# A hybrid decoder layer on one core: the transfers of a block inversion, side by side and on other queues

## The chip, the cores and the metric

One Trainium2 chip, one of its cores. The metric is the device time of one execution in microseconds (us), lower is better. All data are float32; a product of large matrices is done as three float32r products of parts that are split beforehand into a high and a low half.

## The reference, cut to what matters

One decoder layer runs for a prompt of 256 tokens and for 8 samples of 8 tokens each (320 columns together): adaLN modulation from `w_ada`, one input projection, a gated DeltaNet group and an S5 group beside each other, a GLU on the S5 group, one output projection `w_out`, and a SwiGLU FFN. The change touches the DeltaNet group. There, for each of two chunks of 128 tokens (`c`) and 8 heads, a strictly lower triangular matrix `lmat` is built and the unit lower triangular matrix is inverted:

```
lmat = where(strict, einsum('nbhik,nbhjk->nbhij', kb, kc) * decay, 0)
tinv = triangular_solve(eye + lmat, eye, left_side=True, lower=True)
u = einsum('nbhij,nbhjv->nbhiv', tinv, vc * bc)
```

The heads' outputs are normed, gated by `silu(z)`, and go as the first eight of sixteen row blocks into the product with `w_out`; the other eight come from the S5 group through the GLU.

## The kernel before, in words

**The main stream.** TensorE runs a list of segments. A segment is one weight tile of 512 KB: `load` (L467) brings it in through SP's queue, `do_split` (L496) makes its high half `whi` on ScalarE (L501) and its low half `wlo` on VectorE (L502), and `mm3` (L504) does three products for each of its row blocks. Twelve buffers hold the raw tiles and the halves; at most four segments are split ahead. Segments of `w_ada` (tile `ps_ax`) are used unsplit and are mixed in. In the stretch around the change the list holds, in this order: the GLU with part of `w_ada`; the first half of `w_out` (`first_pair`, `first_half`, the S5 blocks, tile `hT`); then the second half of `w_out` (`second_half`, L2209, the DeltaNet blocks, tile `hz`), which starts only when all eight heads are split (`split_head`).

**The background.** Everything else is written as Python generators that run while the list is put out: after each row block of a segment, `tick` lets every background generator go one step. The order of instructions on each engine is the order in which they are put out, so it is set when the program is built, by a clock of the planner's own: `_run` (L180) books each instruction with a cost, `_dma` (L474) books a transfer with 0.47 us of its queue on SP, 0.1 us on ACT and 1.0 us on POOL and with a time at which it lands, and `fits` (L168) holds a background instruction back until, by these booked times, its inputs are ready. `_start` (L151) gives the time from which an instruction may begin; for an output it also takes the last write of the same tile by another engine, and a DMA counts as another engine. A DMA into a tile that an earlier DMA wrote is therefore put out only when the earlier one has landed by the plan.

**The inversion** (`invert`, L1727) is one of these generators. It runs after the head matrices `L` are built, beside the samples (`samples`, one or two heads at a time). It copies the 32 x 32 diagonal blocks of `L` into `Tc` and sends them to a DRAM scratch `dL`, and zeros to the scratches `dT` and `dW` (6 transfers). Then it reads the 16 x 16 blocks back, regrouped, into `Y` (8 transfers of 16 partitions), solves 128 such blocks at once on VectorE in 15 steps (tiles `P`, `X`, L1770), stores `Y` and `X` to `dW` and `dT` (16 transfers), and loads these as `Wc` and `Tc` (4 transfers). All 34 go through SP's queue, among the weight loads. From there the inverse is put together on TensorE from many 32 x 32 and 64 x 64 products (tiles `ps_bA`, `ps_bB`). Then `chunks` runs for the eight heads, and when these and the samples are done, `split_head` makes `hz`. The inversion holds 7 of the 12 buffers `xw` while it runs.

**What shares the engines it uses.** ScalarE makes the halves `whi`, takes the GLU's gates out of PSUM (`gt`), and serves the samples (`sP`, `kr`, `dk`) and the `w_ada` results (`adaev`). GpSimd (POOL) makes the samples' masks `Z` and `sP` and sums squares (`sqa`).

Of the kernel before, what the change touches and what calls it, by code (L numbers as in the profile page):

```python
# [110 lines left out]
class Layer:  # L111
# [36 lines left out]
            e += x * (n - 1)  # L148
        return [(nm, i) for i in range(f // g, e // g + 1)]

    def _start(self, eng, outs, ins, same):  # L151

        t = 0.0
        rd, la = self.rd, self.la
        for ap in ins:
            for k in self._keys(ap):
                r = rd.get(k)
                if r:
                    t = max(t, r[0] + (same if r[1] == eng else 0.2))
        for ap in outs:  # L160
            for k in self._keys(ap):
                for r in (rd.get(k), la.get(k)):
                    if r and r[1] != eng:
                        t = max(t, r[0] + 0.2)
                t = max(t, self.war.get(k[0], 0.0) + 0.2)
        return t

    def fits(self, eng, outs, ins):  # L168

        c = self.clk  # L170
        t = self._start(eng, outs, ins, 0.0)
        if eng == "PE":
            return t <= c["now"] + self.EPS_PE
        return (eng == "SP" or c[eng] <= c["now"] + self.LIM) and t <= max(c[eng], c["now"]) + self.EPS
# [505 lines left out]
    def xw(self, name="xw"):  # L680
        return self._slot(self.mp.tile([128, 356], F32, name=name, tag="xw", bufs=self.CAP["xw"]), "xw", self.CAP["xw"])

    def dma(self, out, in_, eng=None):
        n = 1
        for d in out.shape:
            n *= d
        q = "SP" if eng in (None, self.nc.sync) else "ACT" if eng is self.nc.scalar else "POOL"
        if self.dry:
            self.sig = q, (out,), (in_,)
            return  # L690
        self.stage_end = max(self.stage_end, self._dma(q, n, out, in_))
        return (eng or self.nc.sync).dma_start(out, in_)
# [1034 lines left out]
    def invert(self):  # L1727

        nc, V, G = self.nc, self.V, self.G
        L = self.L  # L1730
        q_ = nc.sync
        yield from self.take("xw", 7)
        yield from self.take("t4")
        v = lambda t: t[:, :256].rearrange("p (h q) -> p h q", h=8)
# [1 line left out]
        dL, dT, dW = (self.dp.tile([4, 32, 16, 32], F32, name="inv%d" % i) for i in range(3))  # L1736
        Tc = [self.xw("Tc") for _ in range(2)]
        Wc = [self.xw("Wc") for _ in range(2)]
# [7 lines left out]
        yield  # L1746
        flat = lambda d: d.rearrange("b r (c h) q -> c (b r) (h q)", c=2)
        for c in range(2):
            yield from self.p.dma(flat(dL)[c], Tc[c][:, :256], q_)
            for d in (dT, dW):  # L1750
                yield from self.p.dma(flat(d)[c], Wc[0][:, :256], q_)
        G.memset(X[:, 0:256:17], 1.0)
        G.memset(T, 0.0)
        yield
# [1 line left out]
        Yv = Y[:, :256].rearrange("p (r q) -> p r q", r=16)  # L1756
        blk = lambda d, s, b: d[b, 16 * s:16 * s + 16, :, 16 * s:16 * s + 16].rearrange("r h q -> h r q")
        for s in range(2):
            for b in range(4):
                p0 = 64 * s + 16 * b  # L1760
                yield from self.p.dma(Yv[p0:p0 + 16], blk(dL, s, b), q_)
        yield
        yield from self.p.ts(Y[:, :256], Y[:, :256], -1.0, OP.mult)
        for i in range(1, 16):
# [10 lines left out]
        for t, d in ((Yv, dW), (Xv, dT)):  # L1775
            for s in range(2):
                for b in range(4):
                    p0 = 64 * s + 16 * b
                    yield from self.p.dma(blk(d, s, b), t[p0:p0 + 16], q_)
        yield  # L1780
        for t, d in ((Wc, dW), (Tc, dT)):
            for c in range(2):
                yield from self.p.dma(t[c][:, :256], flat(d)[c], q_)
        yield
        Pt = [X, Y]

# [868 lines left out]
```

## Time and profile before

| | |
|---|---|
| median of 3 runs | 1825.05 us |
| lowest, highest | 1821.77, 1828.55 us |
| the profiled execution's own time | 1823.18 us |
| its span, first to last instruction | 1821.4 us |
| TensorE matmul busy | 1731.8 us, 95% of the span |
| VectorE, ScalarE, GpSimd busy | 987.7, 768.9, 335.0 us |
| mean granted TensorE clock | 0.977 of full |

The profile is of one execution. Busy times overlap between engines. Where a view says that an engine waited for "issue", it waited for nothing that the profile shows. A matmul's own duration is longer than its share of TensorE's time, because matmuls are pipelined; a product of 320 columns starts each 0.15 us or so while its row says 0.31 us. SPq, ACTq and a POOL row with DMA_DIRECT2D are instructions that start a transfer; their duration is the issue, not the transfer.

### The profile page before, as it was taken

The page shows a single profiled execution, that of the slowest core. Times are in us where ns is not written, and L with a number is a line of the kernel's source. Part 1 is how long each engine was busy: PE and PEld are TensorE (multiplying, and loading weights), DVE is VectorE, ACT ScalarE, POOL GpSimd, SP SyncE. Part 2 cuts the span into 40 slices and gives each one's busy share as a digit, 9 for nine tenths or more (in the row PEclk, how much of TensorE's full clock was granted, in tenths as well). Part 3 has the DMA queues.
Part 4 walks back from the last instruction along what each step waited for, and adds up shares of the span by engine and source line. Part 5 has one row for each costly group of instructions (what it writes and reads, how often), then busy time and mean ns, then how long its engine had stood idle before and what let it go on. Part 6 is the DMA issues. An engine that isn't in the chain of part 4 may idle for free.

```text
span 1821.4 us, 32727 instructions
## 1 busy us (share of the span) xinstructions
PE 1731.8 (95%) x12961; PEld 1600.4 (88%) x12961; DVE 987.7 (54%) x1840; ACT 768.9 (42%) x1439; POOL 335.0 (18%) x439
## 2 busy tenths in 40 slices
PE   7899998898999889997999999999999999999997
PEld 4678997776787769995999999999999999999997
DVE  3587842788865556677633434444443444444455
ACT  3433334677744434664433333333333333333343
POOL 1000185556132212065300000000000000000043
PEclk8999998999999989998999999999999999999998
DMA  8898744776858956758465565554565545655452
GB/s 275 297 369 287 193 111 129 230 217 209 262 172 257 301 172 179 225 165 289 128 185 174 150 183 169 149 150 122 153 176 151 151 119 152 180 150 149 117 154 80
DMA packets 501262, 340.66 MB, mean 187 GB/s; under 512 B 45355, under 2 KB 452619, under 8 KB 500781
## 3 DMA queue, kind: packets, MB, share of 16 engines
q1 hardware_dynamic: 483904, 332.41, 59.5%
q10 hardware_dynamic: 16838, 5.93, 1.3%
q8 instruction: 102, 1.67, 0.4%
q14 instruction: 50, 0.41, 0.1%
q0 software_dynamic: 368, 0.24, 0.1%
HBM read 323.22 MB, written 14.54 MB: 185 GB/s over the span
## 4 chain that ended last, share of the span: by engine, by line
PE 67%; DVE 3%; ACT 1%; issue 1%; DMA 1%; ACTq 0%; SPq 0%; DVEq 0%
PE ps_mm L319 34%; PE ps_bA L319 17%; PE ps_bB L319 14%; PE ps_ax L319 2%; DVE acc L281 1%; DVE wlo L502 1%; PE ps_bA L333 1%; ACT hT L264 0%; DVE u L281 0%; PE ps_mm L333 0%; DVE P L281 0%; DMA inv<-Y 0%; DMA raw<-in_w_ada_dram 0%; ACT whi L501 0%; DMA S<-in_state_delta_dram 0%
## 5 line engine op out<-in xcount | busy, mean ns | idle before, releaser
L502 DVE TENSOR_TENSOR wlo<-raw,whi 128x1024 fp32r<-128x1024 f32 (+2 forms) x441 | 502.6, 1142 | 554.3 <-ACT whi L501 327.2
L501 ACT ACTIVATE whi<-raw 128x1024 fp32r<-128x1024 f32 (+2 forms) x441 | 424.4, 965 | 412.3 <-DVE wlo L502 309.4
L319 PE MATMUL ps_mm<-h,whi 128*128 128x320 f32 x1376 | 303.4, 308 | 0.0
L319 PE MATMUL ps_mm<-hT,whi 128*128 128x320 f32 x1204 | 290.6, 328 | 2.9 <-ACT hT L264 1.5
L319 PEld LDWEIGHTS ps_mm<-h,whi 128*128 128x128 f32 x1376 | 229.9, 187 | 0.8 <-issue 0.8
L319 PEld LDWEIGHTS ps_mm<-hT,whi 128*128 128x128 f32 x1204 | 202.8, 193 | 14.9 <-issue 6.2
L319 PE MATMUL ps_mm<-h,wlo 128*128 128x320 f32 x688 | 211.6, 307 | 0.0
L319 PE MATMUL ps_mm<-hT,wlo 128*128 128x320 f32 x602 | 189.2, 314 | 2.2 <-DVE wlo L502 2.2
L319 PE MATMUL ps_bA<-h,whi 128*128 128x320 f32 x736 | 166.3, 313 | 3.2 <-DVE h L281 3.0
L319 PE MATMUL ps_bB<-h,whi 128*128 128x320 f32 x704 | 156.0, 309 | 0.0
L319 PE MATMUL ps_mm<-f,whi 128*128 128x320 f32 x704 | 155.5, 308 | 0.0
L281 POOL TENSOR_TENSOR sqa<-acc 128x320 f32<-128x320 f32 x1 | 0.7, 722 | 841.1 <-DVE acc L281 841.1
L319 PEld LDWEIGHTS ps_bA<-h,whi 128*128 128x128 f32 x736 | 125.9, 192 | 4.5 <-DVE h L281 3.3
L319 PEld LDWEIGHTS ps_mm<-h,wlo 128*128 128x128 f32 x688 | 128.9, 187 | 0.0
L319 PEld LDWEIGHTS ps_bB<-h,whi 128*128 128x128 f32 x704 | 118.4, 189 | 0.8 <-issue 0.8
L319 PEld LDWEIGHTS ps_mm<-hT,wlo 128*128 128x128 f32 x602 | 115.5, 192 | 3.5 <-DVE wlo L502 3.5
L319 PEld LDWEIGHTS ps_mm<-f,whi 128*128 128x128 f32 x704 | 117.3, 187 | 0.8 <-ACT whi L501 0.8
L319 PE MATMUL ps_bA<-h,wlo 128*128 128x320 f32 x368 | 115.1, 313 | 1.7 <-DVE wlo L502 1.7
L319 PE MATMUL ps_mm<-f,wlo 128*128 128x320 f32 x352 | 108.5, 308 | 0.4 <-DVE wlo L502 0.4
L319 PE MATMUL ps_bB<-h,wlo 128*128 128x320 f32 x352 | 108.6, 308 | 0.0
L319 PE MATMUL ps_ax<-raw,cs 128*32 128x512 f32 (+2 forms) x832 | 99.6, 588 | 6.9 <-DMA raw<-in_w_ada_dram 6.9
L319 PE MATMUL ps_mm<-hx,whi 128*128 128x320 f32 x328 | 81.1, 333 | 3.3 <-ACT whi L501 3.3
(594 smaller groups left out, 2900.7 us busy)
## 6 DMA issues: line engine op xcount, KB each, us to landing
raw<-in_w_ada_dram SPq DMA_DIRECT2D x180, 512.0 KB
raw<-in_w_gate_dram SPq DMA_DIRECT2D x88, 512.0 KB
raw<-in_w_up_dram SPq DMA_DIRECT2D x88, 512.0 KB
raw<-in_w_in_dram SPq DMA_DIRECT2D x66, 512.0 KB
raw<-in_w_down_dram SPq DMA_DIRECT2D x64, 512.0 KB
raw<-in_w_out_dram SPq DMA_DIRECT2D x32, 512.0 KB
raw<-in_w_down_dram SPq DMA_DIRECT2D x64, 192.0 KB
raw<-in_w_glu_dram SPq DMA_DIRECT2D x16, 512.0 KB
```

The costliest lines, as they stand in the source:

```text
L281: return e.tensor_tensor(out, a, b, op=op)
L319: return self.T.matmul(out, lhsT, rhs, start=start, stop=stop)
L333: return self.T.transpose(out, in_, self.ident[b:b + p, b:b + p])
L501: return (self.S.activation(s.hi[:, :w], s.raw[:, :w], AF.Copy), self.V.tensor_tensor(s.lo[:, :w], s.raw[:, :w], s.hi[:, :w].bitcast(F32), ...
L502: self.V.tensor_tensor(s.lo[:, :w], s.raw[:, :w], s.hi[:, :w].bitcast(F32), op=OP.subtract))
```

## The change

The `beside` flag of a transfer takes one rule out of the planner: its output need not wait for the landing of an earlier DMA into the same tile. All 34 transfers of `invert` get it. The six first transfers and the sixteen stores are issued by ScalarE (`qs`), the eight loads of `Y` stay on SP (`q_`), and the four last loads are issued by GpSimd (`ql`). No arithmetic, no transfer and no buffer is added or taken away.

```
-    def _start(self, eng, outs, ins, same):
+    def _start(self, eng, outs, ins, same, dma=False):
...
-                    if r and r[1] != eng:
+                    if r and r[1] != eng and not (dma and r[1] == "DMA" and r is rd.get(k)):
...
     def fits(self, eng, outs, ins):
         c = self.clk
-        t = self._start(eng, outs, ins, 0.0)
+        dma = eng[-1] == "*"
+        eng = eng.rstrip("*")
+        t = self._start(eng, outs, ins, 0.0, dma)
...
-    def dma(self, out, in_, eng=None):
+    def dma(self, out, in_, eng=None, beside=False):
...
-            self.sig = q, (out,), (in_,)
+            self.sig = q + "*" * beside, (out,), (in_,)
...
-        q_ = nc.sync
+        q_, qs, ql = nc.sync, nc.scalar, nc.gpsimd
...
-            yield from self.p.dma(flat(dL)[c], Tc[c][:, :256], q_)
+            yield from self.p.dma(flat(dL)[c], Tc[c][:, :256], qs, beside=True)
             for d in (dT, dW):
-                yield from self.p.dma(flat(d)[c], Wc[0][:, :256], q_)
+                yield from self.p.dma(flat(d)[c], Wc[0][:, :256], qs, beside=True)
...
-                yield from self.p.dma(Yv[p0:p0 + 16], blk(dL, s, b), q_)
+                yield from self.p.dma(Yv[p0:p0 + 16], blk(dL, s, b), q_, beside=True)
...
-                    yield from self.p.dma(blk(d, s, b), t[p0:p0 + 16], q_)
+                    yield from self.p.dma(blk(d, s, b), t[p0:p0 + 16], qs, beside=True)
...
-                yield from self.p.dma(t[c][:, :256], flat(d)[c], q_)
+                yield from self.p.dma(t[c][:, :256], flat(d)[c], ql, beside=True)
```

## Rows read from the trace of the kernel before

**Rows 1.** The page: busy time by engine, and the chain that ended last by engine.
```profile
PE 1731.8 (95%) x12961; PEld 1600.4 (88%) x12961; DVE 987.7 (54%) x1840; ACT 768.9 (42%) x1439; POOL 335.0 (18%) x439
...
PE 67%; DVE 3%; ACT 1%; issue 1%; DMA 1%; ACTq 0%; SPq 0%; DVEq 0%
```

**Rows 2.** Windows (us: length, PE PEld DVE ACT POOL busy; clock, DMA share, GB/s).
```profile
560.00:580.00 20.00, 19.62 (x148) 15.52 (x148) 10.28 (x23) 9.98 (x17) 4.42 (x8) 1.00 0.96 302
580.00:600.00 20.00, 18.82 (x131) 14.93 (x130) 14.62 (x40) 5.53 (x8) 5.52 (x8) 1.00 0.97 322
600.00:620.00 20.00, 18.01 (x137) 14.94 (x139) 8.35 (x23) 8.77 (x15) 4.79 (x8) 1.00 0.88 270
...
640.00:660.00 20.00, 16.42 (x338) 12.95 (x338) 14.16 (x30) 10.86 (x20) 4.57 (x6) 1.00 0.89 280
660.00:680.00 20.00, 14.94 (x413) 13.40 (x414) 9.53 (x26) 4.19 (x12) 2.92 (x7) 0.74 0.33 95
```

**Rows 3.** Waits of PE, 550 to 770 us (total, times, longest).
```profile
PE ps_bB L319 <- issue: 8.0, 2, 4.7
PE ps_mm L333 <- ACT gt L264: 3.1, 2, 1.7
...
PE ps_bA L319 <- DMA S<-in_state_delta_dram: 0.3, 1, 0.3
```

**Rows 4.** The scratch tiles `inv`: issue times ns min/median/max, first and last start.
```profile
L692 SPq DMA_DIRECT2D Y<-inv x8: 328/528/1863, 559.5 to 579.2; - x8
L692 SPq DMA_DIRECT2D inv<-Y x8: 327/644/1988, 601.1 to 626.8; - x8
L692 SPq DMA_DIRECT2D inv<-X x8: 423/559/1892, 627.7 to 642.1; - x8
...
L692 SPq DMA_DIRECT2D Wc<-inv x2: 376/526/675, 642.9 to 643.7; - x2
L692 SPq DMA_DIRECT2D Tc<-inv x2: 320/372/424, 646.7 to 647.1; - x2
```

**Rows 5.** Timeline of DVE, 556 to 603 us (start, duration).
```profile
585.69 1.23 DVE L502 TENSOR_TENSOR wlo<-raw,whi 128x1024 fp32r<-128x1024 f32 x1 [0.94 <-ACT whi L501]
586.83 0.29 DVE L299 TENSOR_SCALAR Y<-Y 128x256 f32<-128x256 f32 x1
...
600.68 0.39 DVE L274 COPY Y<-X 128x256 f32<-128x256 f32 x1
```

**Rows 6.** The tile `Wc`, its first use on PE.
```profile
L319 PE MATMUL ps_bA<-Wc,L x128: 191/191/212, 648.2 to 649.3; 32*32 32x32 f32 x128
```

**Rows 7.** The head tiles `hz`: first products, and their low halves on DVE.
```profile
L319 PE MATMUL ps_mm<-hz,whi x256: 307/308/387, 769.1 to 826.5; 128*128 128x320 f32 x128
...
L281 DVE TENSOR_TENSOR hz<-z,hz x8: 481/484/485, 764.6 to 768.9; 128x320 fp32r<-128x320 f32 x8
```

**Rows 8.** Transfers issued by ACT, of the tiles `so` and `co`.
```profile
L692 ACTq DMA_DIRECT2D out_dram<-so x6: 337/355/437, 498.0 to 503.6; - x6
...
L692 ACTq DMA_DIRECT2D out_dram<-co x12: 746/804/872, 337.1 to 490.4; - x12
```

**Rows 9.** Timeline of ACT, 556 to 602 us, with the idle time before.
```profile
568.34 0.31 ACT L264 ACTIVATE sP<-kr 64x128 f32<-64x128 f32 x1 [5.19 <-PE ps_bA L319]
...
601.76 0.31 ACT L264 ACTIVATE sP<-kr 64x128 f32<-64x128 f32 x1 [5.11 <-issue]
```

**Rows 10.** Timeline of POOL at the start: transfers that it issues.
```profile
1.32 0.71 POOL L560 DMA_DIRECT2D vr<-in_b_ada_dram  x1 [0.86 <-DVE wr L562]
...
2.52 0.49 POOL L566 DMA_DIRECT2D wr<-in_g_post_mix_dram  x1
```

**Rows 11.** Windows of 4 us after the stop in the inversion's products.
```profile
660.00:664.00 4.00, 1.51 (x127) 1.37 (x128) 0.00 (x0) 0.00 (x0) 0.00 (x0) 0.64 0.98 282
664.00:668.00 4.00, 1.80 (x29) 1.32 (x28) 1.31 (x4) 0.00 (x0) 0.00 (x0) 0.50 0.19 53
668.00:672.00 4.00, 4.00 (x27) 3.80 (x26) 3.93 (x11) 0.39 (x1) 0.00 (x0) 0.58 0.00 0
```

## The prediction, made before the changed kernel was run

> **What bounds the kernel now.** I read the page first: TensorE's matmuls cover 95% of the span, and the chain that ended last is 67% TensorE, 1% DMA [rows 1]. So a change that moves no product can pay only where TensorE stands still or runs at a lower clock. The windows show how much that is around the change: in the five that stand there (of the stretch 560 to 680 us, less 620 to 640) TensorE is busy 19.62, 18.82, 18.01, 16.42 and 14.94 of 20 us, 12.2 us short together [rows 2]. Next I asked what TensorE waited for between 550 and 770 us. The longest is "issue", 8.0 us in two stops, then a gate on ScalarE with 3.1 us; the only DMA in the list is a state load of the samples with 0.3 us, and neither a scratch tile of the inversion nor a weight tile stands there [rows 3]. So the inversion's transfers are slow, but TensorE does not wait for them: it has the GLU and the first half of `w_out` to do.
>
> How slow, the tile's own view says: eight loads of `Y` spread over 19.7 us (559.5 to 579.2), sixteen stores over 41.0 us (601.1 to 642.1), four loads to 647.1 [rows 4]; the first product that uses them starts at 648.2 [rows 6]. And who waits for the end of it: the heads' tiles `hz`. Their last low half is made from 768.9 to 769.4 us, and the first product with `hz` starts at 769.1 [rows 7]. The heads are ready in the moment in which TensorE gets to them. Making them earlier makes nothing earlier unless TensorE also gets there earlier.
>
> **The change, part by part.**
>
> *The eight loads of `Y`, let go side by side.* By the median issue of 0.528 us they take 8 x 0.528 = 4.2 us [rows 4], from 559.5 to 563.7. Before, the last issue (579.2) was 7.6 us ahead of the first VectorE instruction on `Y`, at 586.8 [rows 4, 5]; with the same distance the solve starts at 571.3, 15.5 us earlier. On TensorE that is worth nothing. The risk is that VectorE stands at this instruction, because the plan takes it as ready sooner than the queue, full of weights, delivers; behind it in VectorE's order stand the `wlo` halves, 1.23 us each [rows 5]. Bounds: 0 to 3 us lost. I take 0, since the 7.6 us before held other VectorE work and no stop that reached TensorE.
>
> *The solve* is unchanged: 586.8 to 601.1, 14.2 us [rows 5], so now to 585.5.
>
> *Sixteen stores (and the six first transfers) through ScalarE.* What SP is rid of, 22 issues of some half a microsecond, gains nothing, as no weight tile is waited for [rows 3]. What ScalarE gets is 16 issues in a row in the GLU. ScalarE's own transfers took 0.355 us (`so`, whole rows) and 0.804 us (`co`) [rows 8], the same stores on SP 0.644 and 0.559 us with a backlog in the queue, at least 0.327 [rows 4]. So 16 x 0.355 = 5.7 to 16 x 0.804 = 12.9 us; I take 0.5 us, nearest to SP's smallest values and `so`, and get 8 us. In this time ScalarE makes no `whi` and takes no gate out of PSUM. The cover can be read: ScalarE stood still for 5.19 us before 568.34 and for 5.11 us before 601.76 [rows 9], and TensorE's list of waits has nothing that answers to these. ScalarE is otherwise light here, 5.53 of 20 us busy [rows 2]. So about 5 us are hidden: 8 - 5 = 3 us would show if the stores came in one block; the plan puts some other ScalarE work between them, since it lets ScalarE run only about 1 us ahead of its clock. I take 2 us. Bounds: 5.7 - 5 = 0.7, and with breaks nothing, to 12.9 - 5 = 7.9 us.
>
> *The four last loads through POOL.* POOL's issues took 0.49 to 0.71 us [rows 10], four of them 2.0 to 2.8, against 1.8 on SP by its medians (2 x 0.526 + 2 x 0.372) [rows 4]: no difference by itself. What counts is the wait. They must wait for the landing of the stores, POOL works in order, and behind them stand the samples' masks, for which TensorE's sample products wait. And the inversion's first product on TensorE, placed by the plan, then stands in front of all the GLU's products if `Wc` is late. The plan books 0.1 us for a ScalarE issue, so 1.6 us for sixteen, where I expect 8: `Wc` and `Tc` come some 6 us later than the plan has them. Part of that TensorE has already lost at ScalarE (2 us), and the real clock runs behind the plan's: a product of 320 columns is booked with 0.136 us and takes 0.148. Over the 29 us between the first load of `Y` and the end of the stores that gives back 29 x 0.09 = 2.6 us. Left is 6.4 - 2 - 2.6 = 1.8 us; I take 1. Bounds: 0 to 12.9 - 1.6 = 11.3 us.
>
> *The products of the inversion, moved.* With stores from 585.5 to 593.5, some 3 us of landing, 2 us of loads and 1.5 us until use, the first product comes at about 600 us instead of 648.2, and all that follows it about 45 us earlier. The products are the same, and so, I think, is their stop: twice TensorE waited for "issue" in a run of 256 tiny products, and then it ran at a clock of 0.64, 0.50 and 0.58 (half speed is 1.2 instead of 2.4 GHz) for the next 12 us [rows 3, 11]. The DMA share is 0.89 around the stop before and 0.97 and 0.88 around the new place [rows 2], so I see no reason for it to shrink. I take 0. Bounds: the stop goes, -8.0 us, and with it the low clock: the busy 1.51 + 1.80 + 4.00 = 7.3 us at a mean of 0.57 would be 7.3 x 0.43 = 3.1 us shorter, so -11.1; or a third stop, +4.7 [rows 3].
>
> *The heads, 45 us earlier.* Their chains and the samples fill other gaps of TensorE's order; the seven `xw` buffers come free sooner, so two samples run together earlier. `hz` would be ready in the 730s, and TensorE still gets to it when the first half of `w_out` is through, near 770. What the earlier end gives is slack, 0 us.
>
> **The sum**, against the profiled execution's own 1823.18 us (span 1821.4, 1.8 us around it): 0 + 0 + 2 + 1 + 0 + 0 = +3, so 1826 us. The profiled execution is 1.9 us below the median of the runs and inside their spread of 1821.77 to 1828.55, so I leave it there.
>
> **Rivals.**
>
> *The stop in the tiny products goes or shrinks*: 1823.2 - 11.1 = 1812 us. For it: the first run of 128 tiny products at 648.2 had no stop, it is over by 649.5 [rows 6]; where the runs fall between the other products is new. Against it: the two stops came in runs that are put out in one piece, and they still are. Chance 0.18.
>
> *Slower: TensorE stands in front of `ps_bA<-Wc,L`.* One mechanism: ScalarE's issues take 0.8 us as `co` did, the stores end 11.3 us after the plan's time, POOL holds the loads that long, and TensorE, in order, waits. It costs 11.3 us and then the low clock that followed 8.0 us of stops, 3.1 us: 1823.2 + 14.4 = 1838 us. It decides from about 0.6 us an issue on (16 x 0.6 = 9.6, more than the 5 us of cover and the 2.6 us of drift together). For it: the stores are 16 partitions in pieces of 64 bytes, not whole rows. Against it: SP issued the same pieces in 0.33 to 0.42 us at best [rows 4], and ScalarE's own queue holds no weights. Chance 0.18.
>
> *POOL's loads are held up by VectorE.* If each of the four has to wait out one `wlo`, the longest thing VectorE does there, it is 4 x 1.23 = 4.9 us [rows 5] in front of TensorE: 1828 us. No row of before shows POOL issuing beside such work. The Trainium skill ("SBUF — State Buffer", "SBUF: two separate sides") says that GpSimd cannot write the descriptors of its transfers while VectorE holds the port that the two share, and that such a transfer took 3100 ns instead of 620; by an estimate from these figures the four would come 4 x 2.5 = 10 us late. Chance 0.05.
>
> *The transfers are late anyway.* The 16 DMA engines are 96 and 97% busy here, at 302 and 322 GB/s [rows 2]; if the loads and stores wait behind weights, they end little earlier and the plan's order changes without effect: 1823 us. The Trainium skill ("DMA: Bandwidth & Descriptors", "Issuing engines are not separate DMA queues") says that transfers started by different engines run on the same 16 DMA engines, and that more issuing engines save issue time alone. Against it: most of the 41 us of the stores is the plan's spacing, 16 issues by their medians are 8 x 0.644 + 8 x 0.559 = 9.6 us [rows 4]. Chance 0.15.
>
> **How the numbers follow.** The forecast has 0.44, with a range of its own of 1819 to 1833. About 0.5%, 9 us, is what a measurement of this kernel can tell from no change. The first rival is faster by more than that (0.18), the second slower by more (0.18); the forecast, the third and the fourth lie within (0.64). The range goes from 1814, near the first rival's time, to 1836, near the second's.
>
> **What would show it.** Right: no wait of TensorE on `Wc` above 2 us; the first `ps_bA<-Wc,L` near 600 us; `hz` made some 30 us or more ahead of its first product; that product still near 770. ScalarE's issues: 0.36 to 0.6 us each, with PE waiting for `whi` or `gt` 2 to 3 us more than before. The stop for "issue", two times 3 to 5 us, at the new place. Wrong: the stop gone (then the first rival), a wait of 5 us or more on `Wc` or on a mask (the second or third), the first product on `Wc` not before 630 us (the fourth), or the first product on `hz` well away from 770 for a reason not in this list.

## The result, and the profile after

The kernel after takes 1836.07 us (median of 14 runs, 1829.92 to 1847.01), the one before 1823.85 us in the same measurement (14 runs, 1816.45 to 1828.55): ratio 1.007, interval [1.0054, 1.0087]. It is 12.2 us (0.7%) slower, where the forecast was +3 us and a change of less than 0.5%, and lies at the upper end of the range of 1814 to 1836. The profiled execution of after took 1837.29 us, with a span of 1835.5 us.

The page of after, busy time and chain by engine, against [rows 1]:

```profile
PE 1736.9 (95%) x12961; PEld 1602.8 (87%) x12961; DVE 987.5 (54%) x1840; ACT 770.2 (42%) x1441; POOL 333.8 (18%) x443
...
PE 75%; DVE 8%; DMA 6%; POOL 4%; ACT 4%; issue 2%; SPq 1%; ACTq 0%; DVEq 0%; POOLq 0%
```

The instruction counts of TensorE and VectorE are the same. TensorE is busy 5.1 us longer, and the ledger below puts that to the low clock; the span grew by 14.1 us, so it also stood still for longer. The transfers themselves did what the change says. The scratch tiles `inv` in after (issue times in ns, first and last start), against [rows 4], and the first use of `Wc` with the heads' products, against [rows 6, 7]:

```profile
L694 SPq DMA_DIRECT2D Y<-inv x8: 303/447/521, 565.2 to 569.6; - x8
L694 ACTq DMA_DIRECT2D inv<-Y x8: 309/432/671, 585.4 to 591.7; - x8
L694 ACTq DMA_DIRECT2D inv<-X x8: 309/460/594, 592.2 to 597.7; - x8
...
L694 POOL DMA_DIRECT2D Wc<-inv x2: 538/578/617, 603.7 to 604.3; - x2
L694 POOL DMA_DIRECT2D Tc<-inv x2: 538/538/538, 604.9 to 605.5; - x2
```
```profile
L321 PE MATMUL ps_bA<-Wc,L x128: 191/191/212, 609.2 to 610.3; 32*32 32x32 f32 x128
```
```profile
L321 PE MATMUL ps_mm<-hz,whi x256: 304/308/387, 780.6 to 840.3; 128*128 128x320 f32 x128
...
L283 DVE TENSOR_TENSOR hz<-z,hz x8: 481/482/484, 746.5 to 749.3; 128x320 fp32r<-128x320 f32 x8
```

Sixteen stores start within 12.3 us instead of 41.0, the first product on `Wc` comes 39 us earlier, and the heads are ready at 749.8 us. But TensorE gets to them at 780.6 instead of 769.1: they now lie ready for 31 us. Where TensorE lost this is in its list of waits, 550 to 770 us, against [rows 3]:

```profile
PE ps_bA L321 <- DVE kr L301: 9.5, 3, 8.5
PE ps_bA L321 <- issue: 3.0, 2, 2.6
PE ps_bA L321 <- DVE L L283: 2.3, 2, 1.8
PE ps_mm L321 <- DVE wlo L504: 1.4, 2, 0.7
PE ps_mm L335 <- ACT gt L266: 0.8, 1, 0.8
```

One stop of 8.5 us is new. Its chain is read backwards through three timelines (start, duration, idle time before and what ended it): TensorE waits for `kr`, VectorE makes `kr` from `ps_bA`, by a factor for which it waits for `sP` on ScalarE, and ScalarE is issuing stores.

```profile
589.61 0.44 PE L335 MATMUL ps_bA<-ident,xcat 128*128 128x128 f32 x2
...
590.63 0.31 PE L321 MATMUL ps_mm<-hT,wlo 128*128 128x320 f32 x1
599.39 1.19 PE L321 MATMUL ps_bA<-sP,kb 128*128 128x128 f32 x4 [8.46 <-DVE kr L301]
```
```profile
588.27 0.22 DVE L283 TENSOR_TENSOR Z<-xcat,sx 128x64 f32<-128x64 f32 x1
598.64 0.60 DVE L301 TENSOR_SCALAR kr<-ps_bA,dk 64x128 f32<-64x128 f32 x2 [10.15 <-ACT sP L266]
```
```profile
586.15 0.43 ACT L266 ACTIVATE gt<-ps_mm 128x320 f32<-128x320 f32 x1
586.38 5.75 ACTq L694 DMA_DIRECT2D inv<-Y  x6
592.17 5.95 ACTq L694 DMA_DIRECT2D inv<-X  x8
598.23 0.38 ACT L266 ACTIVATE sP<-ps_bA 128x256 f32<-128x256 f32 x1 [11.65 <-DMA raw<-in_w_ada_dram]
```

Fourteen stores stand in one piece in ScalarE's order and hold it for 11.74 us. The mean of 0.84 us from one start to the next hides how: one row lasts 0.31 to 0.67 us, and between some of the rows ScalarE stood still. The timeline, asked for 586.3 to 590 and for 590 to 592.1 us, shows the longest of these standstills, 2.8 us after the fifth of the sixteen stores:

```profile
586.38 1.61 ACTq L694 DMA_DIRECT2D inv<-Y  x3
590.83 1.31 ACTq L694 DMA_DIRECT2D inv<-Y  x3
```

Three more, of 0.25, 0.75 and 1.42 us, stand ahead of the 12th to the 14th store. The four make 5.2 of the 11.74 us; the fourteen issues by themselves take 0.46 us each. No row of ScalarE says what it waited for, but the queues show what was moved meanwhile (packets, MB, share of the 16 DMA engines; q1 holds what SP issued, q10 what ScalarE issued), from 585.4 to 588.5 and from 588.5 to 590.83 us:

```profile
q1 hardware_dynamic: 726, 1.26, 105.8%
...
q1 hardware_dynamic: 715, 0.62, 78.2%
q10 hardware_dynamic: 1360, 0.08, 39.7%
```

All sixteen stores are 4352 packets, so five are 1360. While weights filled the DMA engines, nothing of the five issued stores was moved, and ScalarE issued the sixth when all of the five had been. The same is seen in e4 and e6 below (2.8 and 3.2 us after the fifth store, on again behind 1360 packets) and in e3 (1.9 us after the sixth, on again behind 1632, which is six stores). In e1 and e5 SP issued the sixteen 0.49 us apart without a standstill; there SP had issued no weight tile for 5.2 us before them, and the DMA engines were 30% busy (e1, 586 to 592 us). So the rows put the standstills down to stores that could not move, and not to the price of an issue. No run removes the standstills alone, and why ScalarE stops at five or six is not shown.

The view says that `sP` waited for a weight tile; that is the last semaphore it saw, and the rows above it show what filled the time. What the stop did to the clock is in the windows of 4 us (length, PE PEld DVE ACT POOL busy; clock, DMA share, GB/s), against [rows 11]:

```profile
588.00:592.00 4.00, 2.94 (x32) 2.28 (x30) 0.46 (x3) 0.00 (x0) 0.00 (x0) 1.00 1.06 290
592.00:596.00 4.00, 0.00 (x0) 0.00 (x0) 0.00 (x0) 0.00 (x0) 0.00 (x0) 0.66 1.04 268
596.00:600.00 4.00, 0.61 (x3) 0.64 (x4) 0.60 (x2) 0.38 (x1) 0.00 (x0) 0.50 1.02 286
600.00:604.00 4.00, 4.00 (x19) 4.00 (x19) 0.77 (x2) 0.83 (x3) 1.87 (x3) 0.56 0.48 134
...
628.00:632.00 4.00, 3.82 (x135) 3.42 (x135) 1.81 (x5) 3.80 (x11) 1.21 (x5) 0.50 0.84 233
632.00:636.00 4.00, 4.00 (x34) 3.67 (x34) 0.86 (x4) 1.03 (x3) 0.52 (x1) 0.50 0.30 107
636.00:640.00 4.00, 4.00 (x33) 2.15 (x35) 1.64 (x2) 1.43 (x2) 1.04 (x3) 0.50 0.34 85
```

Half clock (0.50, so 1.2 GHz) until about 603 us behind the stop, and again from 628 to 640, behind the products of the inversion.

**A ledger.** From the first copy into `Tc` to the last product on `hz` TensorE has the same products to do in every kernel here. I cut this stretch into windows of 2 us and added up, in each, idle time (length less PE busy) and low clock (PE busy times one less the granted clock). What is left, the work at full clock, is 253.5 us before and 253.6 after.

| stretch | before: length, idle, clock | after: length, idle, clock |
|---|---|---|
| copy to first product on `Wc` | 93.9, 6.5, 0.0 | 52.7, 10.1, 2.1 |
| the inversion's products | 35.0, 8.4, 2.9 | 34.7, 5.5, 6.7 |
| to the first product on `hz` | 85.9, 0.5, 0.0 | 136.7, 3.4, 0.0 |
| products on `hz` | 57.7, 0.6, 0.0 | 60.0, 2.8, 0.0 |
| sum | 272.5, 16.1, 2.9 | 284.1, 21.8, 8.8 |

The 11.6 us more of this stretch are 5.7 of idle time and 5.9 of low clock. The piece on ScalarE is 8.5 + 2.1 = 10.6 of it; the products lose 12.2 instead of 11.3; the heads' stretch loses 2.2 more; the rest is some 2 better. Whether that makes the piece the cause is what the experiments were for.

### The profile page after: what moved, and what is told of

Same layout as the page of the kernel before. It is cut to its first block, busy times and chain, and to the rows that moved or that the text cites. A ratio compares the mean times of both kernels' runs of the same rounds, so it can differ in the third digit from the quotient of the medians.

```text
span 1835.5 us, 32725 instructions
## 1 busy us (share of the span) xinstructions
PE 1736.9 (95%) x12961; PEld 1602.8 (87%) x12961; DVE 987.5 (54%) x1840; ACT 770.2 (42%) x1441; POOL 333.8 (18%) x443
## 4 chain that ended last, share of the span: by engine, by line
PE 75%; DVE 8%; DMA 6%; POOL 4%; ACT 4%; issue 2%; SPq 1%; ACTq 0%; DVEq 0%; POOLq 0%
PE ps_mm L321 37%; PE ps_bA L321 20%; PE ps_bB L321 15%; PE ps_ax L321 2%; POOL bx L283 2%; DVE wlo L504 2%; DVE ca L308 1%; ACT whi L503 1%; DMA raw<-in_w_out_dram 1%; POOL AB L283 1%; DMA raw<-in_w_in_dram 1%; DMA ts<-ts 1%; POOL ctab L283 1%; PE ps_bB L335 1%; SPq L474 1%
```

## The experiments

Each was timed in five rounds beside the kernel before, whose median was 1821.7 to 1824.1 us from one measurement to the next; so the differences are to be compared, not the medians. "Stretch" is the length of the ledger's stretch in its one profiled execution, "excess" its idle time and low clock.

| run | median, us | above before, us | ratio, interval | stretch less 272.5 | excess |
|---|---|---|---|---|---|
| after | 1836.07 | +12.2 | 1.007 [1.0054, 1.0087] | +11.6 | 21.8 + 8.8 |
| e1 all on SP | 1831.61 | +9.2 | 1.0049 [1.0036, 1.0061] | +8.0 | 21.5 + 4.9 |
| e2 queues, no flag | 1835.99 | +13.6 | 1.0079 [1.0059, 1.0099] | +8.4 | 20.9 + 4.8 |
| e3 issue booked | 1834.70 | +12.3 | 1.0064 [1.0045, 1.0083] | +12.2 | 22.5 + 9.0 |
| e4 last loads on SP | 1845.31 | +22.9 | 1.0124 [1.0098, 1.0151] | +24.0 | 28.8 + 14.3 |
| e5 held, SP | 1840.85 | +16.8 | 1.0098 [1.007, 1.0125] | +14.1 | 20.0 + 11.4 |
| e6 held, ScalarE | 1838.71 | +14.7 | 1.0084 [1.0056, 1.0113] | +15.3 | 25.3 + 8.6 |
| e7 before, 16 cuts | 1830.77 | +6.7 | 1.0043 [1.0026, 1.0059] | +4.7 | 16.3 + 1.7 |
| e8 chunks held | 1832.58 | +8.5 | 1.005 [1.0031, 1.0069] | +9.6 | 22.2 + 7.7 |
| e9 after's plan, SP | 1832.86 | +9.8 | 1.0049 [1.0032, 1.0066] | +9.2 | 19.4 + 9.1 |
| e10 before's plan, new queues | 1827.08 | +4.0 | 1.0019 [1.0008, 1.003] | +4.5 | 17.8 + 6.3 |
| e11 control | 1823.72 | +0.7 | 1.0 [0.9984, 1.0016] | +0.8 | 15.4 + 4.8 |
| e12 one step | 1827.70 | +4.7 | 1.0018 [1.0002, 1.0034] | +2.4 | 14.5 + 7.9 |
| e13 three queues | 1830.94 | +7.2 | 1.0046 [1.0029, 1.0064] | +10.4 | 17.4 + 12.7 |
| e14 pairs, ScalarE | 1823.63 | -0.1 | 1.0004 [0.9989, 1.0019] | +0.4 | 16.3 + 3.3 |
| e15 before, 2 pieces | 1823.84 | +0.1 | 1.0004 [0.9991, 1.0017] | +0.4 | 15.7 + 3.7 |
| e16 before, 4 pieces | 1827.62 | +3.9 | 1.002 [1.0007, 1.0033] | +3.6 | 16.6 + 4.4 |
| e17 e13, products later | 1834.69 | +13.0 | 1.0072 [1.0056, 1.0087] | +12.5 | 19.8 + 10.8 |
| e18 pairs, SP | 1837.75 | +16.0 | 1.0084 [1.0057, 1.0111] | +10.6 | 22.1 + 5.2 |

In 13 of the 19 kernels the stretch gives the difference of the medians within 1.2 us, in the others within 2.0 to 5.4; so most of the difference is made there. (It is one execution of each. That of the control e11 was 7.7 us above the median of its runs, and its stretch only 0.8 us longer than that of before: the scatter of a kernel lies mostly elsewhere.)

**First: take ScalarE or POOL out (e1 to e4).**

e1: `q_, qs, ql = nc.sync, nc.sync, nc.sync`

> The changed kernel with all 34 transfers back on SP's queue, still let go side by side. Theory A (fourteen stores in one piece hold ScalarE for 11.7 us, a sample's eviction stands behind them, TensorE waits 8.5 us for it and then runs at half speed): the wait on kr is gone, time within 4 us of the kernel before, 1820 to 1828. Theory B (the early place of the inversion, beside the GLU, costs by itself; the queue does not matter): 1833 or more. Theory C (the loads through POOL, whose wait holds up masks): gone too, 1820 to 1828, told from A by the run with the loads alone on SP. The 2.3 us lost in the second half of w_out should stay under B and under A alike if they come from heads that are ready early.

e2: the kernel after with `, beside=True` taken from all 34 calls.

> The changed kernel without the side-by-side rule: stores still through ScalarE, last loads through POOL, each transfer spaced by the landing of the one before. Theory A: single stores of 0.4 to 0.8 us between other ScalarE work hold nothing up, so 1820 to 1828, first product on Wc near 640 us as in the kernel before. Theory B: also 1820 to 1828. Theory C: a loss stays if POOL's wait is the cause, over 1828.

e3, in `dma`, ahead of `_dma`:
```
+        if beside and q == "ACT":
+            self.clk[q] = max(self.clk[q], self.clk["now"]) + 0.7
```


> The changed kernel with ScalarE's issues booked by the plan at 0.8 us from its clock's now, instead of 0.1 us from wherever ScalarE's clock stood: the sixteen stores are spread over some 13 us of the plan, 7 and 9 with a whi and a gate between. Theory A: the eviction no longer stands behind fourteen of them at once, the 8.5 us wait shrinks to 0 to 4 us, 1822 to 1831. Theory B and C: 1833 or more.

e4: `q_, qs, ql = nc.sync, nc.scalar, nc.sync`

> The changed kernel with only the four last loads back on SP. Theory A and B: no change against the changed kernel, 1832 to 1840. Theory C: the loss is gone, 1820 to 1828.

The stop for `kr` was gone in e1, as it should be; the time came back by 3.0 us only (+9.2 in place of +12.2), between the ranges of A and B, since TensorE then waited 3.7 us for `Tc<-inv`, and the stretch to the heads lost 8.1 us. e3 gave ScalarE's issues a price in the plan: no stop for `kr` above 0.6 us, and the same time as after, against theory A. e4 acquits POOL: with its loads on SP the stop is still there (8.6 us) and the time is worse. In e2 the stores were spread again (616.8 to 664.6 us) but late, the heads' low halves were begun until 779.3, behind the first product on `hz` at 775.2, and TensorE waited 1.4 us for them: the zero slack of [rows 7] is real. The products on `hz` lost 5.9 us there in place of 0.6, of which some 2.8 are seen with early heads too. The piece alone does not explain the time.

**Second: hold the products back (e5, e6, e8).** e5 is e1, e6 is after, each with the first line ahead of `Pt = [X, Y]` in `invert`; e8 is e1 with it behind `invert()`. `y5r` is the S5 group's norm, ready when the GLU is through.
```
+        while self.y5r is None:
+            yield
```


> All transfers side by side on SP, and the inversion's products held back until the GLU's norm is made (near 648 us, where they stood in the kernel before). Theory Early (inversion and head chains beside the GLU are what costs 7 to 9 us): 1820 to 1826, the idle time and low clock of TensorE between the first copy and the last product on hz back to 17 to 21 us from 26.4. Theory Order (any new order that the plan writes costs some us, the kernel before has a lucky one): 1827 to 1834.

> The changed kernel, stores through ScalarE and loads through POOL as changed, with the same hold. Theory Block (fourteen stores in one piece cost 10.6 us by themselves) with Early: the wait on kr near 590 us stays at 7 to 9 us, time 1830 to 1836, about 10 above the held kernel on SP. Early alone: like the held kernel on SP, 1820 to 1826. Order alone: 1832 to 1840.

> All transfers side by side on SP, the inversion's products early, only the heads' chains held back until the GLU's norm is made. If the chains beside the GLU are what costs (Early, chains): 1821 to 1827. If the products beside the GLU do (Early, products), or Order: 1828 to 1834.

None came back to the kernel before. e5 is above the ranges of both its theories; e6 lies in that of Order alone, with its stop for `kr` still there (8.8 us); e8 lies in that of Order or the products. So neither the early products nor the early chains are what costs: held (e5, e6, e8) or not (e1, after), the excess is 26 to 34 us.

**Third: order and queue apart (e9 to e12).** The planner's booking and the real queue can be separated, because `dma` gets both from one argument. In e9 the plan is that of after, instruction for instruction on TensorE, VectorE and POOL, but SP really issues:
```
+        if beside and eng is self.nc.scalar:
+            eng = self.nc.sync
         return (eng or self.nc.sync).dma_start(out, in_)
```


> The planner books everything as in the changed kernel, so TensorE, VectorE and POOL run the changed kernel's order instruction for instruction, and ScalarE its order less 22 issues; only those 22 transfers are really issued by SP. Theory Block (the 14 issues that stood in one piece on ScalarE cost the 8.5 us stop and the 2.1 us of low clock behind it): the stop goes, at least 8 of the 10.6 us come back, 1824 to 1828 us, no lasting difference from the kernel before. Theory Order (the new order of the products costs by itself): TensorE stands as long elsewhere, 1831 to 1836 us. Third: the stores wait on SP behind weight loads, then TensorE waits for Wc and the time is above 1836 us.

e10 is the converse: `dma(..., q_, real)` books SP as before and issues by `real or eng`, ScalarE for the 22 transfers and POOL for the last four.

> The converse: every compute engine runs the order of the kernel before, and only the queues are those of the change (22 transfers issued by ScalarE, the four last loads by POOL, each at its old place in the program). Theory Order: between the old plan's other ScalarE work the 16 issues are spread over some 40 us, no stop above 2 us, 1822 to 1828 us. Theory Block in its wide form (any issue on ScalarE costs 0.8 us of TensorE, in a block or not): 16 x 0.8 = 12.8 us, 1832 to 1838 us.

e11: `dW, dL, dT = (self.dp.tile(...` in the kernel before.

> The kernel before with its three scratch tiles allocated in another order: the same instructions in the same order on every engine. It says what two programs of one order may differ by. All theories: 1821 to 1827 us, within 0.2% of the kernel before. If it is off by 0.4% or more, time depends on something other than order and queues, and none of the small differences of this study counts.

e12: one `yield` behind `flat = ...` in the kernel before.

> The kernel before with one more step of its background loop ahead of the inversion's first transfers: no queue, no transfer and no rule is changed, but the order of the products behind it is. Theory Order (the order of the kernel before happens to fit, and most others cost idle time and low clock): 1828 to 1836 us. Theory that only the transfers and their queues cost: 1821 to 1827 us.

The control came out at 1.0: two programs of one order show no difference, and its interval, 0.16% or 2.9 us to either side, says how small a difference still counts. In e9 the time is that of theory Order. The stop for `kr` went, and another came (TensorE's waits, SP's queue and VectorE's timeline of e9):

```profile
PE ps_bA L321 <- DVE X L283: 6.1, 1, 6.1
```
```profile
586.37 5.60 SPq L696 DMA_DIRECT2D inv<-Y  x8
592.07 5.03 SPq L696 DMA_DIRECT2D inv<-X  x8
...
598.25 0.45 SPq L474 DMA_DIRECT2D raw<-in_w_glu_dram  x1
```
```profile
605.62 1.23 DVE L504 TENSOR_TENSOR wlo<-raw,whi 128x1024 fp32r<-128x1024 f32 x1 [8.58 <-DMA raw<-in_w_ada_dram]
```

The sixteen stores take 10.7 us of SP instead; SP issues no weight tile between 586.3 and 598.2 us, VectorE stands 8.58 us at a `wlo` whose tile comes late, and the `X` that TensorE wants is behind it. So in this order the piece has a price on either queue, and it is paid by what stands behind it. Of the 12.2 us it gave back 2.4; the excess of the products rose from 12.2 to 18.5 us.

In e10 ScalarE issued the stores between its other work, one to four at a time, each in 0.31 us (`Y`, median) or 0.46 (`X`). TensorE's longest stop for ScalarE was 2.1 us, and 3.1 us went to the low clock ahead of the products (0.0 before, 1.7 in the control): +4.0 us, at the upper end of theory Order's range. The inversion's stores and TensorE's waits, 550 to 770 us:

```profile
L692 ACTq DMA_DIRECT2D inv<-Y x8: 309/310/685, 604.0 to 625.4; - x8
L692 ACTq DMA_DIRECT2D inv<-X x8: 309/458/770, 625.9 to 646.2; - x8
```
```profile
PE ps_bB L319 <- issue: 7.2, 2, 4.1
PE ps_mm L333 <- ACT gt L264: 3.1, 2, 1.7
PE ps_bA L319 <- ACT kr L264: 2.1, 1, 2.1
```

And e12, which changes no queue and no transfer, cost 4.7 us by the medians, with an interval that begins at 0.02%. That lies between the ranges of its two theories; still, moving the order by one step may be worth as much as the queues.

**Fourth: break the piece up (e13, e14, e17, e18).** e13 keeps the plan of after and lets three engines issue in turn; e14 keeps ScalarE and puts steps of the loop behind every second store:
```
# e13, in dma
+        if beside and eng is self.nc.scalar:
+            self.nst = getattr(self, "nst", -1) + 1
+            eng = (self.nc.scalar, self.nc.sync, self.nc.gpsimd)[self.nst % 3]
# e14, in invert, behind each store
+                    if b % 2:
+                        for _ in range(6):
+                            yield
```


> The order of the changed kernel on TensorE and VectorE, with its 22 transfers issued in turn by ScalarE, SP and POOL, so that each queue has a third of the piece, some 4 us. Theory Piece (11 to 12 us in one queue are what TensorE waits for, whichever queue): the stops for kr (8.5 us) and X (6.1 us in e9) both go or are below 2 us, 1824 to 1829 us. Theory Order: the stops shrink, but the time stays at 1831 to 1836 us since the rest of the order costs as much.

> The changed kernel with six steps of the background loop behind every second store, all on ScalarE as in the change: ScalarE's other work goes between pairs, so no piece is above some 3 us. Theory Piece: no stop for kr above 2 us, 1824 to 1829 us, about the kernel before. Theory Order: a new order like all the others, 1828 to 1836 us, without the stop.

In e13 the stops for `kr` and `X` were below 2 us, although ScalarE still stood still for 2.9 us ahead of the last of its six stores; the products then lost 12.7 us to the low clock. TensorE's waits, 557 to 643 us:

```profile
PE ps_bA L321 <- issue: 3.2, 1, 3.2
...
PE ps_bA L321 <- DVE kr L301: 1.9, 2, 1.6
PE ps_bA L321 <- DMA Wc<-inv: 1.9, 1, 1.9
```

e14 is level with the kernel before, about as theory Piece had it. ScalarE's order there (timeline) has the stores in twos and fours between its work, and TensorE's waits, 550 to 770 us, show what is left:

```profile
583.14 0.91 ACTq L694 DMA_DIRECT2D inv<-Y  x2
586.91 0.38 ACT L266 ACTIVATE sP<-ps_bA 128x256 f32<-128x256 f32 x1 [3.82 <-DMA inv<-Y]
589.11 0.27 ACT L266 ACTIVATE kr<-ps_bA 64x128 f32<-64x128 f32 x1 [1.81 <-DVE kr L283]
589.17 0.81 ACTq L694 DMA_DIRECT2D inv<-Y  x2
```
```profile
PE ps_bA L321 <- issue: 3.2, 3, 2.4
PE ps_mm L335 <- ACT gt L266: 2.9, 2, 1.5
PE ps_bA L321 <- DVE kr L301: 2.1, 4, 0.7
PE ps_bA L321 <- DMA Wc<-inv: 1.6, 1, 1.6
```

Two runs asked what e13 had still lost. e17 is e13 with `for _ in range(40): yield` ahead of the first product; e18 is e14 with all three queues set to SP.

> e13 with 40 steps of the background loop between the last four loads and the first product, so the transfers lie early and side by side on three queues, and the products stand about where e14 has them (620 to 660 us). Theory Place (what e13 still lost is idle and low clock where the products stand early): these fall from e13's 18.2 us to 9 to 12, and the time to 1822 to 1828 us. If the shared queues cost it, or a new order does: 1829 to 1834 us.

> e14 (six steps behind every second store) with all 34 transfers on SP's queue, as in the kernel before. Theory Piece: which queue doesn't matter once the piece is broken up, 1821 to 1827 us, within 0.2% of the kernel before. If ScalarE's queue was needed for that (weights wait behind stores on SP): 1828 to 1834 us.

Theory Place and theory Piece both fell. e17 put the products where e14 has them (625.4 to 662.5 us) and they lost 6.4 + 9.1 us there, so the early place was not the reason; and in e1 and e8, where they begin earliest (596.6 and 595.0 us), they lost 10.9 and 11.1, no more than the 11.3 of the kernel before. e18 has no long piece and no issue on ScalarE, its longest waits are those of the kernel before ("issue" 6.0 us, `gt` 3.3), and it is 16 us slower. So a broken piece alone does not bring the time back; that e14's order is also one of those that fit is the likely reading, and is not shown.

**Fifth: the tiny products' own stop (e7, e15, e16).** One step after each head (e7), after the first chunk (e15: `if not c: yield`) or after every fourth head (e16: `if h % 4 == 3 and (c, h) != (1, 7): yield`) in the run of 256 products of the kernel before.

> The kernel before with one change: the run of 256 tiny products is broken up, sixteen of them at a time with the main stream between. Theory that the stop for issue comes from running through more small instructions than can be brought up: both stops (8.0 us) and the low clock after them (2.9 us) go, 1811 to 1816. If the stop has another cause: 1820 to 1826.

> The kernel before, with one step of the loop between the first and the second chunk's 128 tiny products. If the stop of TensorE (8.0 us, and 2.9 us of low clock) belongs to runs of 256 and not of 128, it goes with hardly any interleaving, 1812 to 1817 us. If it stays, 1822 to 1827 us. Theory Order: the shift behind it costs 3 to 9 us, 1826 to 1832 us, whatever the stop does.

> The same in four pieces of 64 tiny products. If the stop goes and the interleaving costs in proportion to the cuts (5.7 us for 16 cuts in e7, so some 1.4 us), 1813 to 1819 us; Theory Order: 1826 to 1832 us.

The waits for "issue" from 650 to 704 us in e7 fell from 8.0 to 1.8:

```profile
PE ps_bB L319 <- issue: 1.2, 1, 1.2
...
PE ps_mm L319 <- issue: 0.6, 1, 0.6
```

The excess of the products went from 11.3 to 2.5 us, as hoped. But the work at full clock rose from 253.5 to 259.2 us, the stretch behind lost 6.1 instead of 0.5, and the heads 2.8 instead of 0.6: 4.7 us more in the stretch, 6.7 by the medians. In two or four pieces the stop shrank less (5.3 and 4.5 us) and the time did not fall. No version in this study beats the kernel before.

## Why the prediction was wrong, point by point

**What bounds the kernel** was read rightly: TensorE does, it waited for no transfer, and the heads had no slack to give. "The heads are ready in the moment in which TensorE gets to them" held in both directions: 31 us of earliness earned nothing, and TensorE waited for late heads (e2).

**Loads of `Y` and the solve**: the spread of the loads was right (4.4 us, 4.2 forecast), and the solve cost TensorE nothing. That its last copy ended at 585.4 us, with 585.5 forecast, is luck in part: the loads began at 565.2 instead of 559.5, and VectorE's first instruction on `Y`, at 571.7, stood 2.1 us behind the last of them instead of 7.6.

**ScalarE's stores, 2 us: the step that failed.** The price of an issue was right, 0.46 us for the 0.5 forecast. The size of the cover, 5 us, was near, and by luck: it was read from idle time ahead of `sP<-kr`, while behind the stores this time stood `sP<-ps_bA`; the product that this one reads ended at 590.05 us, so some 3.5 us after `gt` were free. What the sum put at nothing is that stores which cannot move stop the engine that issues them: 5.2 us of standstill among the 14. The break-up by other work, which was to bring 3 us down to 2, did not come either: the planner books 0.1 us for such an issue, from wherever ScalarE's clock stands, and its limit of about 1 us ahead let 14 go out together. And the sum had no low clock behind the stop. By an estimate from these rows, 14 issues of 0.46 us less 3.5 us of cover would have stopped TensorE for some 3 us; the trace has 8.5 us and 2.1 of low clock, 10.6 in place of 2. The prediction had read that the DMA engines were 96 and 97% busy, but used it only for late transfers, in its fourth rival. As a difference in time the step is worth less: with the same order and the piece taken off ScalarE, 2.4 (e9) and 5.0 us (e13) came back, with intervals that overlap that of after. So the stop is shown to come from the stores; that the 12.2 us do is not.

**POOL's loads, 1 us**: the issues were priced right, 0.54 to 0.62 us each. The 1 us was for a wait on `Wc`, and TensorE does not wait for `Wc` at all; e4 shows that SP does it no better. In the working, the 29 us over which the plan's clock was to drift are 34 by the prediction's own times (559.5 to 593.5); that gives back 3.1 us in place of 2.6 and leaves 1.3 in place of 1.8, and the 1 us would have been the same. The Trainium skill ("SBUF — State Buffer", "SBUF: two separate sides") says that GpSimd cannot write descriptors while VectorE holds their port. In e14 the four loads were issued from 617.34 to 619.55 us beside a `wlo` from 617.78 to 619.01, in 0.54 to 0.62 us each as in after; they landed after 5.5 to 6.1 us instead of 2.8 to 3.6, with the DMA engines full in e14 (617 to 626 us) and 72% busy in after (603 to 609). So no run here shows such a hold, and none rules it out.

**The products, 0 us**: the stop did shrink, from 8.0 to 3.0 us, as the first rival had it, but the clock took it back (6.7 instead of 2.9 us), and their excess is 12.2 against 11.3.

**The heads, 0 us**: 2.2 us more, because TensorE waited for the sums `M` 2.4 instead of 0.5 us in that stretch. Ten of the other kernels show the same 2.8 us of idle time there.

**The rivals.** The second one's condition was met in the mean only (0.84 us an issue, above its 0.6, but 0.46 without the standstills). Its time, 1838, is near by luck. Its place was wrong: it expected TensorE in front of `Wc`, held by POOL; ScalarE's own next instruction stood first. The fourth had the full DMA engines right and their effect wrong: the transfers came early, and the issuing engine paid. What no rival had is that a plan made by a clock is itself a cost: moved by one step it lost 4.7 us by the medians (e12), with the change's plan and the piece off ScalarE 7 to 10 (e9, e13).

**What stays open.** The piece on ScalarE is shown to stop TensorE for 8.5 us, and the excess of the stretch accounts for most of the time. What the other orders lose, and why e14's lets all of it go while e13's, e17's and e18's do not, with no more than six stores in a row in any of them, is not settled; no single wait tells them apart, and their excess lies in many stops of 1 to 4 us with half clock behind some of them.

## What to carry to other kernels

When a compute engine is to issue many transfers in a row, price more than the issues. Ask whether the first of them can move, since a few that wait behind weights held the issuing engine here, and ask which instruction stands behind them in that engine's order: the idle time that another instruction had is not its cover. Where a planner orders the work, changing the price or a rule of one step changes every order behind it; run a control and a one-step shift first, so that the size of this effect is known before small gains are looked for.

## What the runs showed of the hardware

The same 16-partition stores took ScalarE 0.31 to 0.46 us each by their medians when they came one to four at a time (e10; four in a row took 1.81 us). Fourteen in a row took 11.74 us (after): 0.46 us each, and 5.2 us of standstills, the longest behind five stores of which nothing had been moved while the DMA engines were full. On SP sixteen in a row took 7.7 us in e1 and e5, and 10.7 us in e9. Behind 8.5 us without a product TensorE's granted clock was 0.50 until about 4 us after it had begun again (after).
